# A's second score product cut to 64 rows, its two halves on opposite row groups of the array

## The chip, the cores and the metric

One NeuronCore of one Trainium2 chip runs the whole program. The metric is the device time of one execution in microseconds. A run of the same kernel is compared with other runs of it by their median; the profile is of one execution.

## What is computed

A trunk of two encoder layers over 1024 tokens of width 1024. Each layer projects the normalised input, runs three groups of attention heads side by side (A: six dense heads of 64 with two key heads, B: six windowed heads, C: four latent heads), gates their outputs and projects them back. The change lies in group A. Cut to what matters, the reference for it is

```python
def dense_gqa_blocks(q, k, v, scale):        # A: 6 query heads, 2 key heads, head dim 64
    qb = q.reshape(bsz, nb, BLOCK, n_kv, grp, d).transpose(1, 0, 2, 3, 4, 5)
    def one_block(q_blk):                    # 128 queries against all 1024 keys
        s = jnp.einsum('bqhgd,bkhd->bhgqk', q_blk, k).astype(jnp.float32) * scale
        p = jax.nn.softmax(s, axis=-1).astype(v.dtype)
        return jnp.einsum('bhgqk,bkhd->bqhgd', p, v)
```

All values are float32. The kernel splits each operand of a product into a high part in the type fp32r and a low part (what the high part leaves), and adds products of parts.

## The kernel before

**Stages.** Each layer has an input stage (projections, rotations, transposes; queries, keys and gates are written to DRAM), an attention stage, and an output stage. In the profile the attention stages lie at about 277 to 560 us (layer 0) and 921 to 1206 us (layer 1).

**Query stacks.** For group A and a tile of 128 queries, `qstack` (L767) loads one tile of 128 rows from DRAM (`qsta` in the trace) with four DMAs on SP's queue. Of each head, 64 rows hold the high part and the other 64 rows the low part; which half is which depends on whether the head is even or odd. The keys' high part (`ks["a", 0]`) and low part (`ks["a", 1]`, both `ka` in the trace) each hold the 64 rows of a key head twice, in the upper and the lower half.

**A unit.** `UnitA` (L894) is one head and one query tile: 8 query tiles x 2 key heads x 3 heads, 48 in a layer, 96 in all. Its `scores` (L899) handles the 1024 keys in two halves of 512. For a half, `mm3` (L133) issues two products that add up in one PSUM bank: the stack with the high keys (high x high + low x high) and the stack with the low keys (high x low + low x low). Both contract 128 rows. `softmax_unit` (L703) then lets DVE read the bank once (L711: copy with sign and running minimum), and after the second half ACT takes the exponential (L721). The transposes (L730), the split of the result (L737 to L742) and the product with the values (`pv`, L752) follow in later turns of the pipeline (L830).

**Buffers.** Three PSUM banks serve scores (`SBANKS`), four transposes, one the values. Gate tiles (`gt`, L807 and L1115) have `GBUFS` = 5 buffers, the tile `rb` (L791) two: `divided` (L778) makes the reciprocal sums, turns them, copies them to `rb` on ACT and multiplies them into the gate tile on POOL (L794).

**What sets the order.** The tile framework orders each engine's instructions by a timeline of its own, starting from priorities and dependences; `tc.keep_in_program_order` ties single instructions to the order in which they are written. SP's DMA queue is in order: an issue that waits for a buffer holds those behind it.

Of the kernel before, what the change touches and what calls it, by code (L numbers as in the profile page):

```python
# [8 lines left out]
F32 = mybir.dt.float32  # L9
F32R = mybir.dt.float32r  # L10
# [18 lines left out]
QAB = 4  # L29
QC = 4  # L30
OBUFS = 4
GBUFS = 5
C_AT = (2, 3, 5, 6, 8, 9, 11, 13)
WARM = 12
XBUFS = 6
# [10 lines left out]
def kernel(  # L46
# [21 lines left out]
    nc = tc.nc  # L68
    P = 128
# [14 lines left out]
    def after(ins, first):  # L84

        tc.add_manual_dep(
            ins,
            first.name,
            mybir.DependencyInfo(mybir.DependencyClass.NoSync, mybir.DependencyReason.DATA),
            reason="order",  # L90
        )
        return ins

    def dma(dst, src, eng=None):

        a, b = (t.bitcast(F32) if t.dtype == F32R else t for t in (dst, src))
        ins = (eng or nc.sync).dma_start(a, b)
        if queue_behind[0] is not None and eng is None:
            after(ins.ins, queue_behind[0])
        return ins.ins  # L100
# [3 lines left out]
    class Engine:  # L104


        def __init__(self, eng):
            self.eng = eng
# [16 lines left out]
    def rstd_of(ss, n, name, w):  # L125

        ms = small.tile([P, w], F32, tag=f"ms{w}", name=f"ms_{name}")
        V.tensor_scalar(ms, ss, 1.0 / n, EPS, ALU.mult, ALU.add)
        r = small.tile([P, w], F32, tag=f"rs{w}", name=f"rs_{name}")
        last_pow[0] = G.tensor_tensor(out=r, in0=ms, in1=mhalf[:, 0:w], op=ALU.pow).ins  # L130
        return r

    def mm3(ps, parts, first=True, last=True):  # L133

        for i, (a, b) in enumerate(parts):
            T.matmul(ps, lhsT=a, rhs=b, start=first and i == 0, stop=last and i == len(parts) - 1)  # L136
# [91 lines left out]
    for l in range(DEPTH):  # L228
        x_src = xin if l == 0 else x_next[l - 1]
        last = l == DEPTH - 1  # L230
# [4 lines left out]
        d_q = {g: dram.tile([NS, 2, P, 3, P], F32R, name=f"d_q{g}{l}") for g in "abc"}  # L235
# [11 lines left out]
        with stage.ph as ph:  # L247
# [6 lines left out]
            def ps_t(name):  # L254
                return ps1.tile([P, 512], F32, tag="T", name=name)
# [8 lines left out]
            def gemm_sc(ws, st, name):  # L264
                his, los, n = ws
                hf, c0 = st // 4, (st % 4) * P
                ps = ps_o(name)
                for dt in range(ND):
                    wh, wl = his[dt], los[dt]
                    h, lo = hTh[hf][:, dt, c0 : c0 + P], hTl[hf][:, dt, c0 : c0 + P]  # L270
                    mm3(ps[:, :n], [(h, wh), (h, wl), (lo, wh)], dt == 0, dt == ND - 1)
                return ps
# [144 lines left out]
            for st in range(NS):  # L417
                nm = f"{l}_{st}"
                ps = gemm_sc(ws, st, f"pza{nm}")
# [9 lines left out]
                r = rstd_of(ss, 1, f"a{nm}", 8)  # L429
# [31 lines left out]
            for st in range(NS):  # L461
                nm = f"{l}_{st}"
                ps = gemm_sc(ws_b, st, f"pzb{nm}")
# [218 lines left out]
        with ExitStack() as ph:  # L682
            ps2 = wa_.enter_context(tc.tile_pool(name=f"ps2_{l}", bufs=2, space=PSUM, reuse_waits="tile"))
            at = ph.enter_context(tc.tile_pool(name=f"at{l}", bufs=2, reuse_waits="tile"))
# [5 lines left out]
            pk = pk_.enter_context(tc.tile_pool(name=f"pk{l}", bufs=1, side="right", reuse_waits="tile"))  # L690
# [3 lines left out]
            def ps_s(name):  # L694
                return ps2.tile([P, 512], F32, tag="S", name=name, bufs=SBANKS)
# [4 lines left out]
            def ps_o(name):  # L700
                return ps2.tile([P, 512], F32, tag="O", name=name, bufs=OBANKS)

            def softmax_unit(half, sm, nm):  # L703


                nmx = [small.tile([P, 1], F32, tag=f"nmx{c}", name=f"nmx{nm}_{c}") for c in range(2)]
                p = at.tile([P, 1152], F32, tag="p", name=f"p{nm}", bufs=PBUFS)[:, 0:1024]
                for c in range(2):
                    ps = ps_s(f"s{nm}_{c}")
                    half(ps, c)  # L710
                    V.tensor_tensor_reduce(  # L711
                        p[:, c * 512 : (c + 1) * 512],
                        ps,
                        zero[:, 0:1].to_broadcast([P, 512]),
                        -1.0,
                        nmx[0][:, 0:1] if c else 3.0e38,
                        ALU.add,
                        ALU.min,
                        nmx[c],
                    )  # L720
                A.activation(p, p, AF.Exp, scale=-1.0, bias=nmx[1][:, 0:1], accum_out=sm)  # L721
                return p

            def transposed(p, pth, ptl, g, kts, nm, pool=True):

# [41 lines left out]
            def qstack(g, qt, nm):  # L767

                qcnt[0] += 1
                i = qcnt[0] % QAB  # L770
                t = (pk if i in (1, 2) else pq).tile([P, 6, P], F32R, tag=f"qst{i}", name=f"qst{nm}")
                t = t.rearrange("p (m a) s -> p m a s", a=2)
                for par, i in ((0, 0), (0, 1), (1, 0), (1, 1)):
                    r0 = 64 * (par ^ i)
                    ins = dma(t[r0 : r0 + 64, :, par, :], d_q[g][qt, i, 64 * par : 64 * par + 64])
                return t, ins

            def divided(gt, sums, n, nm):  # L778

                pr = ps_t(f"pr{nm}")  # L780
                rc = small.tile([P, 3, 2], F32, tag="rc", name=f"rc{nm}")
                V.reciprocal(rc[:, 0:n, :], sums)
                wide = at.tile([P, 384], F32, tag="rw", name=f"rw{nm}", bufs=1)
                G.tensor_copy(
                    wide[:, 0 : n * P].rearrange("p (m a d) -> p m a d", a=2, d=64),
                    rc[:, 0:n, :].unsqueeze(3).to_broadcast([P, n, 2, 64]),
                )
                for m in range(n):
                    ms = slice(m * P, (m + 1) * P)
                    T.transpose(pr[:, ms], wide[:, ms], ident)  # L790
                rb = at.tile([P, 384], F32, tag="rb", name=f"rb{nm}")  # L791
                A.copy(rb[:, 0 : n * P], pr[:, 0 : n * P])
                gv = gt.rearrange("p g s -> p (g s)") if len(gt.shape) == 3 else gt
                G.tensor_tensor(out=gv, in0=gv, in1=rb[:, 0 : n * P], op=ALU.mult)  # L794

            class Gqa:


                def __init__(self, g, qt, m0):
                    self.g, self.qt, self.m0 = g, qt, m0  # L800
                    self.nm = f"{g}{l}_{qt}"
                    self.q, self.loaded = qstack(g, qt, self.nm)
                    self.sm = small.tile([P, 6], F32, tag=f"sm{g}", name=f"sm{self.nm}", bufs=3)
                    self.o = at.tile([P, 3, P], F32, tag="o", name=f"o{self.nm}", bufs=OBUFS)

                def gate(self):
                    self.gt = qg.tile([P, 3, P], F32, tag="gt", name=f"gt{self.nm}", bufs=GBUFS)  # L807
                    dma(self.gt, d_gate[:, self.m0 : self.m0 + 3, self.qt * P : (self.qt + 1) * P])
# [13 lines left out]
                def divide(self):  # L822

                    divided(self.gt, self.sm.rearrange("p (m a) -> p m a", a=2), 3, self.nm)
# [55 lines left out]
            if True:  # L880
                ks, start = {}, {}
# [12 lines left out]
                class UnitA:  # L894
# [4 lines left out]
                    def scores(self):  # L899
                        a, kv, h = self.a, self.kv, 3 * self.kv + self.g  # L900

                        def half(ps, c):
                            cs = slice(c * 512, (c + 1) * 512)
                            mm3(ps, [(a.head(h), ks["a", 0][:, kv, cs]), (a.head(h), ks["a", 1][:, kv, cs])])

                        self.p = softmax_unit(half, a.sm[:, h : h + 1], self.nm)

                    def turn(self):
                        if self.g == 0:
# [180 lines left out]
            class GroupC:  # L1090
# [23 lines left out]
                def gate(self):  # L1114
                    self.gt = qg.tile([P, 384], F32, tag="gt", name=f"gt{self.nm}", bufs=GBUFS)  # L1115
                    dma(self.gt[:, 0 : self.n], d_gate[:, 6 + self.hp, self.q0 * P : self.q1 * P])
# [9 lines left out]
            class UnitC:  # L1126
# [5 lines left out]
                def scores(self):  # L1132
                    ks, par, t = self.c.ks, self.par, self.c.qts[self.g]

                    def half(ps, c):
                        cs = slice(c * 512, (c + 1) * 512)
                        stack, mixed = t[:, 0, par, :], t[:, 1, par, :]
                        mm3(ps, [(stack, ks.k1[:, par, cs]), (mixed, k2[:, par, cs]), (mixed, k3[:, cs])])

                    self.p = softmax_unit(half, self.c.sm[:, par, self.g : self.g + 1], self.nm)  # L1140
# [75 lines left out]
        with ExitStack() as ph:  # L1216
# [10 lines left out]
            for st in range(NS):  # L1227
                nm = f"{l}_{st}"
# [4 lines left out]
                for c in range(2):  # L1233
                    cs = slice(c * 512, (c + 1) * 512)
                    for _ in out_part(st, c, MW if (st, c) in wa_.ps else 0, 8):
                        pass
                    ps = wa_.ps[st, c]
# [16 lines left out]
                if last:  # L1254
                    ms = small.tile([P, 1], F32, tag="ms1", name=f"ms_f{nm}")
                    V.scalar_tensor_tensor(ms, ss[:, 1:2], 1.0 / D, e0, ALU.mult, ALU.add)
                    r = small.tile([P, 1], F32, tag="rs1", name=f"rs_f{nm}")
# [93 lines left out]
```

## Time and profile before

| what | value |
|---|---|
| median of 3 runs | 1325.95 us (1325.19 to 1326.66) |
| the profiled execution | 1325.05 us |
| its span, first to last instruction | 1323.3 us |
| PE busy | 1294.8 us, 98% |
| DVE, ACT, POOL busy | 67%, 54%, 40% |
| mean granted clock of TensorE | 0.996 of full speed |

The page gives for one execution how long each engine was busy, and for groups of instructions the time of one and what ended the idle time before it. PE is the matrix engine, PEld its weight loads, which run beside products. A record of a product runs from its start to its modelled end; the next product may start before that end, so the distance of two starts (the step) is told from the timeline or the chain, not from a record's length. The chain of waits follows the work that ended last back through what released it.

### The profile page before, as it was taken

The numbers are of one execution on the slowest core, as the hardware profiler recorded it, in microseconds if no ns is written. First come the engines' busy times: TensorE is split into PE (matmuls) and PEld (weight loads), VectorE is DVE, ScalarE is ACT, GpSimd is POOL, SyncE is SP. The second block draws the span as 40 slices with busy tenths as digits, with TensorE's granted clock in tenths as the row PEclk, the third lists the DMA queues.
The fourth block names the chain that finished last, engine by engine and source line by source line (L and its number), as shares of the span: only waits on it lengthen the run. The fifth ranks groups of instructions, "written<-read, shape, count | busy, mean of one in ns | idle before, by whom it ended". The sixth has DMA issues, their size and how long they took to land.

```text
span 1323.3 us, 21690 instructions
## 1 busy us (share of the span) xinstructions
PE 1294.8 (98%) x7320; PEld 1131.1 (85%) x7320; DVE 882.6 (67%) x2242; ACT 720.7 (54%) x1551; POOL 530.2 (40%) x602
## 2 busy tenths in 40 slices
PE   7999999999999999999999999999999999999997
PEld 7888998878998998878898889888798988888786
DVE  5685662058888988875537766600888899888543
ACT  4332341168888898842323224311888889887332
POOL 3430121026766666751114101200367776677210
PEclk8999999999999999999999999999999999999999
DMA  7244469255211431345523345791742226114443
GB/s 255 89 125 150 136 203 258 89 140 142 82 49 56 115 90 47 108 144 177 186 91 115 121 134 157 237 221 55 180 102 61 72 64 149 38 40 148 147 146 115
DMA packets 174702, 166.46 MB, mean 126 GB/s; under 512 B 22400, under 2 KB 147200, under 8 KB 174592
## 3 DMA queue, kind: packets, MB, share of 16 engines
q1 hardware_dynamic: 155840, 140.43, 37.3%
q10 hardware_dynamic: 18752, 24.65, 5.4%
q8 instruction: 58, 0.95, 0.3%
q14 instruction: 52, 0.43, 0.1%
HBM read 107.35 MB, written 57.67 MB: 125 GB/s over the span
## 4 chain that ended last, share of the span: by engine, by line
PE 84%; DVE 5%; ACT 4%; DMA 3%; issue 2%; POOL 1%; SPq 1%; POOLq 0%; DVEq 0%; ACTq 0%
PE pg L136 13%; PE pw L136 12%; PE pzb L114 7%; PE pza L114 7%; PE poa L136 6%; PE ppa L730 5%; PE pzc L136 5%; PE sa L136 5%; PE sc L136 4%; PE ppc L730 4%; PE poc L136 3%; PE sb L136 2%; PE pob L136 2%; PE pzv L114 2%; PE pzv L136 2%
## 5 line engine op out<-in xcount | busy, mean ns | idle before, releaser
L711 DVE CUSTOM_DVE_ANT_0 pa<-sa,zero 128x512 f32<-128x512 f32 x96 | 65.5, 682 | 140.2 <-PE sa L136 137.1
L738 POOL TENSOR_SCALAR ptha<-pfa 128x512 fp32r<-128x512 f32 x96 | 59.8, 624 | 207.8 <-ACT pfa L737 199.7
L739 POOL TENSOR_TENSOR ptla<-pfa,ptha 128x512 fp32r<-128x512 f32 x96 | 124.1, 1293 | 5.7
L136 PE MATMUL sa<-ka,qsta 128*128 128x512 f32 x384 | 124.5, 418 | 1.4 <-DVE nmxc L711 0.7
L721 ACT ACTIVATE pa<-pa,nmxa 128x1024 f32<-128x1024 f32 x96 | 111.4, 1161 | 8.8 <-DVE nmxa L711 8.8
L136 PE MATMUL sc<-k,qc 128*128 128x512 f32 x384 | 113.2, 411 | 0.0
L730 PE MATMUL ppa<-ident,pa 128*128 128x128 f32 x768 | 106.5, 273 | 0.2
L730 PEld LDWEIGHTS ppa<-ident,pa 128*128 128x128 f32 x768 | 91.5, 141 | 15.1 <-DVE ptlb L742 0.6
L136 PE MATMUL pw<-woh,oh 128*128 128x512 f32 x256 | 98.9, 395 | 3.4 <-ACT oh L1029 2.6
L136 PE MATMUL pg<-hTh,wh 128*128 128x512 f32 x256 | 100.4, 392 | 0.0
L136 PE MATMUL pg<-hTh,wl 128*128 128x512 f32 x256 | 100.1, 391 | 0.0
L136 PE MATMUL pg<-hTl,wh 128*128 128x512 f32 x256 | 100.1, 391 | 0.0
L136 PE MATMUL pw<-wol,oh 128*128 128x512 f32 x256 | 99.7, 392 | 0.1
L136 PE MATMUL pw<-woh,ol 128*128 128x512 f32 x256 | 97.9, 393 | 0.3 <-DVE ol L1030 0.3
L644 ACT ACTIVATE g<-pg 128x512 f32<-128x512 f32 x32 | 19.1, 598 | 137.3 <-PE pg L136 107.0
L218 POOL TENSOR_SCALAR wh<-wst 128x384 fp32r<-128x384 f32 (+1 forms) x52 | 30.6, 607 | 145.5 <-PE pzb L114 79.2
L136 PE MATMUL poa<-ptha,vAB 128*128 128x384 f32 x256 | 88.0, 344 | 0.9 <-POOL ptla L739 0.3
L136 PE MATMUL poa<-ptla,vAB 128*128 128x384 f32 x256 | 86.5, 338 | 0.0
L721 ACT ACTIVATE pc<-pc,nmxc 128x1024 f32<-128x1024 f32 x64 | 74.0, 1156 | 8.2 <-DVE nmxc L711 8.0
L136 PEld LDWEIGHTS sc<-k,qc 128*128 128x128 f32 x384 | 66.3, 189 | 8.6
L711 DVE CUSTOM_DVE_ANT_0 pa<-sa,zero,nmxa 128x512 f32<-128x512 f32 x96 | 71.2, 744 | 3.4 <-PE sa L136 0.7
L730 PE MATMUL ppc<-ident,pc 128*128 128x128 f32 x512 | 71.9, 273 | 1.5 <-ACT pfc L737 0.8
(234 smaller groups left out, 3812.6 us busy)
## 6 DMA issues: line engine op xcount, KB each, us to landing
wst<-in_w_in_dram SPq DMA_DIRECT2D x20, 512.0 KB, 3.7
d_gate<-g ACTq DMA_DIRECT2D x32, 256.0 KB, 2.0
wost<-in_w_out_dram SPq DMA_DIRECT2D x32, 256.0 KB, 2.7
wst<-in_w_in_dram SPq DMA_DIRECT2D x16, 384.0 KB, 4.2
qsta<-d_qa SPq DMA_DIRECT2D x64, 96.0 KB, 2.8
qstb<-d_qb SPq DMA_DIRECT2D x64, 96.0 KB, 2.8
k<-d_kn SPq DMA_DIRECT2D x12, 512.0 KB, 7.0
qc<-d_qc SPq DMA_DIRECT2D x96, 64.0 KB, 2.2
```

The costliest lines, as they stand in the source:

```text
L114: return lambda *a, **k: tc.keep_in_program_order(f(*a, **k))
L136: T.matmul(ps, lhsT=a, rhs=b, start=first and i == 0, stop=last and i == len(parts) - 1)
L218: G.tensor_scalar(h, f, 1.0, 0.0, ALU.mult, ALU.add)
L644: A.activation(g, ps, AF.Silu)
L711: V.tensor_tensor_reduce(p[:, c * 512 : (c + 1) * 512], ps, zero[:, 0:1].to_broadcast([P, 512]), -1.0, nmx[0][:, 0:1] if c else 3.0e38, AL ...
L721: A.activation(p, p, AF.Exp, scale=-1.0, bias=nmx[1][:, 0:1], accum_out=sm)
L730: T.transpose(pt[:, (j - q0) * P : (j - q0 + 1) * P], p[:, j * P : (j + 1) * P], ident)
L738: G.tensor_scalar(hi, f, 1.0, 0.0, ALU.mult, ALU.add)
L739: G.tensor_tensor(out=lo, in0=f, in1=hi.bitcast(F32), op=ALU.subtract)
```

## The change

The second product of a half keeps only the high rows of the query: 64 rows against the low keys (low x low is left out). The first half of the keys takes the rows where the head's high part lies in the old stack. The second half takes the other 64 rows, for which a second tile, `other` (`qota` in the trace), holds the high parts of the odd and even heads in exchanged halves; two more DMAs per query tile load it, into one of two buffers. Both halves' banks are taken first, and the four products are issued in the order high, high, low, low and tied to it. To make room, gate tiles have four buffers and `rb` one.

```diff
-GBUFS = 5
+GBUFS = 4
...
-            def softmax_unit(half, sm, nm):
+            def softmax_unit(half, sm, nm, both=None):
...
+                if both:
+                    pss = [ps_s(f"s{nm}_{c}") for c in range(2)]
+                    both(pss)
                 for c in range(2):
-                    ps = ps_s(f"s{nm}_{c}")
-                    half(ps, c)
+                    if both:
+                        ps = pss[c]
+                    else:
+                        ps = ps_s(f"s{nm}_{c}")
+                        half(ps, c)
...
+            def ordered(ps, a, b, first, last):
+                tc.keep_in_program_order(nc.tensor.matmul(ps, lhsT=a, rhs=b, start=first, stop=last))
...
-                rb = at.tile([P, 384], F32, tag="rb", name=f"rb{nm}")
+                rb = at.tile([P, 384], F32, tag="rb", name=f"rb{nm}", bufs=1)
...
+                    if g == "a":
+
+                        self.other = pk.tile([P, 3, P], F32R, tag=f"qot{qt % 2}", name=f"qot{self.nm}")
+                        for par in range(2):
+                            r0 = 64 - 64 * par
+                            dma(self.other[r0 : r0 + 64], d_q[g][qt, 0, 64 * par : 64 * par + 64])
...
-                        def half(ps, c):
-                            cs = slice(c * 512, (c + 1) * 512)
-                            mm3(ps, [(a.head(h), ks["a", 0][:, kv, cs]), (a.head(h), ks["a", 1][:, kv, cs])])
-
-                        self.p = softmax_unit(half, a.sm[:, h : h + 1], self.nm)
+                        def both(pss):
+                            cs = [slice(c * 512, (c + 1) * 512) for c in range(2)]
+                            hi, lo = ks["a", 0], ks["a", 1]
+                            for c in range(2):
+                                ordered(pss[c], a.head(h), hi[:, kv, cs[c]], True, False)
+
+                            for c, stack in enumerate((a.head(h), a.other[:, h // 2, :])):
+                                r = slice(64, 128) if (h + c) % 2 else slice(0, 64)
+                                ordered(pss[c], stack[r], lo[r, kv, cs[c]], False, True)
+
+                        self.p = softmax_unit(None, a.sm[:, h : h + 1], self.nm, both)
```

On PE, query tile 4 of layer 0, key head 0, second head of its group, before (a name is stage, tile, key head, head, half and a running number; `ka` with the smaller number is the high part of the keys, and the 512 columns of the result stand last):

```order
L730 MATMUL ppb_3_1_1_0_4721<-ident,scb_3_1_4652 128x128 x3
L136 MATMUL sa_4_0_1_0_4816<-ka_0_2789,qsta_4_4751 128x512
L136 MATMUL sa_4_0_1_0_4816<-ka_0_2792,qsta_4_4751 128x512
L136 MATMUL sa_4_0_1_1_4820<-ka_0_2789,qsta_4_4751 128x512
L136 MATMUL sa_4_0_1_1_4820<-ka_0_2792,qsta_4_4751 128x512
L136 MATMUL sb_4_0_0_4860<-kb_0_2802,qstb_4_4758 128x384
```

and with the change:

```order
L799 MATMUL pra_3_4817<-ident,rwa_3_4820 128x128 x3
L731 MATMUL sa_4_0_1_0_4831<-ka_0_2792,qsta_4_4763 128x512
L731 MATMUL sa_4_0_1_1_4832<-ka_0_2792,qsta_4_4763 128x512
L731 MATMUL sa_4_0_1_0_4831<-ka_0_2795,qsta_4_4763 128x512
L731 MATMUL sa_4_0_1_1_4832<-ka_0_2795,qota_4_4768 128x512
L136 MATMUL poa_3_1_2_4859<-ptha_3_1_0_1_4639,vAB_90 128x384
```

The four products now go high, high, low, low, and the last reads the second tile; other units' work around them moved too. Over the program the two 64-row products stand directly behind each other in 94 of 96 units.

On SP's queue, where the attention of layer 0 begins, before:

```order
L97 DMA qsta_0_2782<-d_qa_78 64x3x128 x4
L97 DMA ka_0_2789<-d_ka_81 64x2x1024 x2
L97 DMA ka_0_2792<-d_ka_81 64x2x1024 x2
L97 DMA qstb_0_2795<-d_qb_79 64x3x128 x4
L97 DMA kb_0_2802<-d_kb_82 64x2x1024 x2
```

and with the change, there and, farther on, at query tile 3:

```order
L97 DMA qsta_0_2782<-d_qa_78 64x3x128 x4
L97 DMA qota_0_2787<-d_qa_78 64x384 x2
L97 DMA ka_0_2792<-d_ka_81 64x2x1024 x2
...
L97 DMA qota_3_4281<-d_qa_78 64x384 x2
L97 DMA qstb_3_4286<-d_qb_79 64x3x128 x3
L97 DMA qc_0_6_4963<-d_qc_80 64x2x128 x2
```

The first two loads of the new tile stand between the query stack and the keys; those of tile 3 stand ahead of loads for groups B and C.

## Rows read from the trace of the kernel before

**Rows 1.** The page: span, share of each engine, and the granted clock in 40 slices.
```profile
span 1323.3 us, 21690 instructions
...
PE 1294.8 (98%) x7320; PEld 1131.1 (85%) x7320; DVE 882.6 (67%) x2242; ACT 720.7 (54%) x1551; POOL 530.2 (40%) x602
...
PEclk8999999999999999999999999999999999999999
```

**Rows 2.** Windows of both attention stretches: length, busy us (x instructions) of each engine, clock, DMA.
```profile
core 0: us, PE busy (x) PEld busy (x) DVE busy (x) ACT busy (x) POOL busy (x), PEclk, DMA share, GB/s
277.00:560.00 283.00, 279.15 (x1749) 248.76 (x1748) 247.84 (x691) 244.89 (x529) 186.66 (x208) 1.00 0.35 91
921.00:1206.00 285.00, 280.99 (x1751) 250.15 (x1750) 242.07 (x682) 241.00 (x521) 184.60 (x205) 1.00 0.33 86
```

**Rows 3.** Tile sa: ns min/median/max, first and last start in us.
```profile
L136 PEld LDWEIGHTS sa<-ka,qsta x384: 186/189/192, 277.0 to 1179.6; 128*128 128x128 f32 x192
L136 PE MATMUL sa<-ka,qsta x384: 387/397/504, 277.2 to 1179.8; 128*128 128x512 f32 x192
L711 DVE CUSTOM_DVE_ANT_0 pa<-sa,zero x96: 649/682/693, 277.9 to 1179.6; 128x512 f32<-128x512 f32 x96
L711 DVE CUSTOM_DVE_ANT_0 pa<-sa,zero,nmxa x96: 731/745/754, 279.2 to 1181.6; 128x512 f32<-128x512 f32 x96
```

**Rows 4.** Timeline around the first attention product: start us, us, engine.
```profile
276.34 0.39 PE L136 MATMUL pg<-hTh,wl 128*128 128x512 f32 x1
276.34 0.19 PEld L136 LDWEIGHTS pg<-hTh,wh 128*128 128x128 f32 x1
276.57 0.39 PE L136 MATMUL pg<-hTh,wh 128*128 128x512 f32 x1
276.57 0.19 PEld L136 LDWEIGHTS pg<-hTl,wh 128*128 128x128 f32 x1
276.79 0.39 PE L136 MATMUL pg<-hTl,wh 128*128 128x512 f32 x1
276.80 0.19 PEld L136 LDWEIGHTS pg<-hTh,wl 128*128 128x128 f32 x1
```

**Rows 5.** Chain of waits, in order of time, of a piece of layer 0's attention.
```profile
427.22 0.46 PE sa L136 x2
...
428.73 0.47 PE sa L136 x2
...
429.54 0.87 PE ppc L730 x8
...
435.25 0.47 PE sa L136 x2
435.72 0.44 PE ppa L730 x4
436.16 0.69 PE sc L136 x3
```

**Rows 6.** Chain of waits by line, in 277 to 560 and in 921 to 1206 us.
```profile
by line: PE poa L136 14.7%; PE ppa L730 10.6%; PE sa L136 10.0%; PE sc L136 9.4%; PE ppc L730 8.0%; PE poc L136 4.6%; PE pob L136 4.5%; DVE pa L711 4.5%; PE sb L136 4.3%; issue 3.4%; PE ppb L730 2.6%; ACT pa L721 2.5%; ACT scb L969 2.2%; DV
...
by line: PE poa L136 15.5%; PE sa L136 11.8%; PE ppa L730 11.6%; PE sc L136 9.0%; PE ppc L730 7.4%; PE poc L136 5.9%; PE sb L136 4.8%; PE pob L136 4.5%; DVE pa L711 3.4%; PE ppb L730 3.2%; PE pg L136 2.5%; issue 2.2%; ACT pa L721 1.6%; DVE 
```

**Rows 7.** Waits of PE in 277 to 560 us: us in total, times, longest.
```profile
PE sb L136 <- DVE nmxa L711: 1.8, 5, 1.0
PE sa L136 <- DVE nmxc L711: 0.4, 1, 0.4
```

**Rows 8.** The page's DMA issues: KB each, us to landing.
```profile
qsta<-d_qa SPq DMA_DIRECT2D x64, 96.0 KB, 2.8
```

**Rows 9.** Tile qsta: its loads as issued on SP's queue.
```profile
L97 SPq DMA_DIRECT2D qsta<-d_qa x64: 512/605/754, 207.1 to 1116.1; - x64
```

**Rows 10.** Tile ka: its loads as issued on SP's queue.
```profile
L97 SPq DMA_DIRECT2D ka<-d_ka x8: 585/605/618, 210.5 to 863.3; - x8
```

**Rows 11.** Waits of SP's queue in 277 to 560 us.
```profile
SPq L97 <- POOL ob L827: 54.7, 7, 14.7
```

**Rows 12.** Tiles gta and rba: gate loads, the copy, the multiplication that reads both.
```profile
L97 SPq DMA_DIRECT2D gta<-d_gate x16: 377/487/1307, 240.7 to 1134.1; - x16
L794 POOL TENSOR_TENSOR gta<-gta,rba x16: 1003/1016/1030, 306.9 to 1198.9; 128x384 f32<-128x384 f32 x16
...
L792 ACT COPY rba<-pra x16: 467/485/523, 306.2 to 1197.4; 128x384 f32<-128x384 f32 x16
```

## The prediction

> **What bounds the kernel now.** I read the page first. TensorE (PE) is busy for 1294.8 of 1323.3 us, 98%; the next engine, VectorE (DVE), for 67% [rows 1]. [...] The change acts in the two attention stretches alone, so I read the windows of those: PE busy 279.15 of 283 us and 280.99 of 285 us, with DVE at 248 and 242 us and ScalarE (ACT) at 245 and 241 us, 85 to 88% [rows 2]. Two more engines stand close behind PE there.
>
> A busy PE says little of what one product is worth, since the records overlap: a score product of A is recorded with 397 ns (median) and its weight load with 189 ns [rows 3], yet in the timeline one 512-column product starts every 0.22 to 0.23 us, and the weight load of the next starts with it and lies beside it [rows 4]. The price of a product is therefore its step, not its record. The chain of waits gives the same: two A products take 0.47 us, so 0.235 each, and eight transposes 0.87 us, so 0.109 each with a weight load of their own [rows 5].
>
> Last, how much of A's product time lies on the path. The chain by line in the two stretches has A's scores (sa) at 10.0% of 283 us and 11.8% of 285 us, 28.3 + 33.6 = 61.9 us [rows 6]. All 384 products at 0.235 us are 90.2 us. So 69% of this work is on the chain; the rest lies beside pieces that DVE, ACT or an issue ends. What PE waits for by name is small, at most 1.8 us in a row of the waits [rows 7].
>
> **The change, part by part.**
>
> *Four steps become three.* Before, a unit (one head, 128 queries, 1024 keys) has two halves of two products. There are 96 units (96 reductions of each half, [rows 3]), so 384 products. After, it still has 384 products and 384 weight loads, but the two second ones of a unit use 64 rows each, on opposite halves of the array, into different banks. If they run side by side, a unit loses one step of 0.235 us. They stand directly behind each other in 94 of 96 units: 94 x 0.235 = 22.1 us of PE time.
>
> No row of this trace shows a 64-row product, so I bound it. More than one step cannot be gained: three passes of 512 columns are left, and no row shows one with a shorter step than 0.22 us. The other end: no overlap, the array running empty before and after the pair (record minus step, 397 - 235 = 162 ns each time) and a weight load of 109 ns not hidden each time: 2 x 271 ns x 96 = +52 us. I take the gaining end, because the nearest row, the back-to-back stream [rows 4], shows that PE starts a product as soon as weights and columns are there, and here neither rows, nor banks, nor a semaphore holds the second one. Weight loads have room: four at 0.109 us are 0.44 us under three steps of 0.705 us.
>
> [...]
>
> *How much of it reaches the end.* Between 69% (the chain's share) and 100% (PE is busy for 98.6% of the stretches). I take 0.8, nearer to the chain's share, since DVE and ACT at 85 to 88% would rise to about 90% in a stretch 9 us shorter. 22.1 x 0.8 = 17.7 us; ends 15.2 and 22.1.
>
> *The order high, high, low, low.* Now a first reduction can start after three steps where it could after two, and the second follows it at once. Per unit: before, 0.47 us of products, then 0.682 + 0.745 us of reductions [rows 3] (the second half's products, done at 0.94 us, hide behind the first reduction); after, 0.705 us and the same reductions. Each unit's exponential comes 0.235 us later. Other products and transposes cover that, except where the chain runs through these reductions: DVE pa has 4.5% and 3.4% of the two stretches [rows 6], 12.7 + 9.7 = 22.4 us, which is 16 units at 1.43 us. 16 x 0.235 = 3.8 us is the upper end, 0 the lower; I take 1 us, since the order was laid anew around it. A unit also holds two of three score banks at once; that is in the same upper end.
>
> *Two more loads per query tile.* 16 query tiles x 2 issues of 96 KB, like those of qsta, which take 2.8 us to land [rows 8] and 0.605 us to issue [rows 9]. That is 32 x 0.605 = 19 us of SP's queue and 3 MB of 166 MB. The queue has room: in the first stretch alone it waits 54.7 us for one kind of store [rows 11]. The first of them stand behind qsta and ahead of ka: qsta and ka are issued from 207 and 210 us [rows 9, 10], the first score product starts at 277 [rows 3], so 1.2 us more is covered by 60. The later ones have two buffers, so a load waits for the last unit of the tile two before, and in the order rows qc and qstb stand behind it on the queue. Those are needed a query tile later, some 35 us (283 us over 8 tiles). Taken at 0. If that cover went, a late landing would cost up to 2.8 us on each of 14 tiles, 39 us; nothing in the rows points to it.
>
> *Four gate buffers, one rb.* The first gate tile is loaded from 240.7 us and first used at 306.9 [rows 12]; one buffer fewer eats into 66 us of lead. The rb copy (485 ns) would wait for the multiplication of the one before (1016 ns [rows 12]), which ended many microseconds earlier: 16 of A over both stretches is one in 35 us. Both 0.
>
> Sum: 1325.05 - 17.7 + 1.0 = 1308.4 us against the profiled execution (span 1323.3 plus 1.75 around it). The median of the runs shown is 0.9 us above that execution, so I forecast **1309 us**; the forecast's own range is 1303 to 1313.
>
> **The rivals.**
>
> *A. The second of the pair waits for its weights.* In all the rows shown a load starts with the product before its own, one ahead and not two [rows 4]. If that always holds, the second 64-row product starts one load, 0.109 us, behind the first; a pair gives 0.126 us, and 94 x 0.126 x 0.8 - 1 = 8.5 us: 1317 us. For it: the rows never show two ahead. Against: they have full-height loads alone, for which there is no free half.
>
> *B. Slower: the array runs empty at each change of height.* A pair stands between 128-row products, so there are two changes per unit. If nothing starts until the last product is out, each costs 397 - 235 = 162 ns at both edges of the pair: +0.324 - 0.235 = +0.089 us per pair, 94 of them 8.4 us, with 1 us for the order: 1334 us. The point from which it decides is 0.118 us a change. For it: each record has 0.16 us of tail to lose. Against: going from products to transposes, another kind of work on the array, costs nothing in the chain (two products 0.47 us, four transposes 0.44, three products 0.69, one behind the other [rows 5]). If the pair moreover doesn't overlap it is 96 x 0.324 + 1 = 32 us, 1357 us, the far tail of this case.
>
> [...]
>
> *C. The change doesn't do what it says.* The two run one after the other, each with a step of its own, and no change costs anything. PE's time stays, the order's 1 us is left: 1326 us.
>
> *D. Another engine takes over.* PE gets its 22 us, but DVE and ACT hold the stretches, and a quarter comes through: -5.5 + 1 = 1320.5 us. For it: 85 to 88% busy. Against: PE's own idle time is only 8 us of 568 now.
>
> **How the numbers follow.** Forecast 0.42, A 0.17, B 0.23, C 0.12, D 0.06. A measurement of this kernel tells about 0.2%, 2.7 us, from no change. Faster by more: forecast, A and D less 0.04 for a smaller A or D, 0.61. Within: that 0.04 and most of C, 0.12. Slower: B and what is left of C, 0.27. Range 1303 to 1337: from the forecast's best end to a little past B; left out are B's far tail (about 0.08) and a better gain than one step (0.03).
>
> **What would show it.** In the changed profile: right, if the two 64-row products of a unit start within some 10 ns of each other, the next product starts about 0.235 us after them, and the two stretches are 7 to 11 us shorter each. A shows as a start 0.11 us behind. B shows as more than 0.3 us between the last 128-row product and the pair, or behind it. C shows as 0.235 us between the two. D shows as a PE with gaps that reductions or ACT end. The forecast is wrong if the time is above 1313 us; the reasoning is wrong if it is below 1303.

## The result, and the profile after

| | before | with the change |
|---|---|---|
| median | 1326.31 us (4 runs, 1325.19 to 1327.38) | 1462.7 us (4 runs, 1461.79 to 1467.17) |
| ratio | 1 | 1.1036, 95% interval 1.1022 to 1.1051 |
| span of the profiled execution | 1323.3 us | 1461.2 us |

The change makes the kernel 136 us slower. The forecast was 1309 us, the range ended at 1337.

The page of the changed kernel: span, engines, granted clock in 40 slices, and the chain by engine.

```profile
span 1461.2 us, 21779 instructions
...
PE 1350.4 (92%) x7320; PEld 1128.6 (77%) x7320; DVE 877.8 (60%) x2242; ACT 726.2 (50%) x1551; POOL 528.6 (36%) x602
...
PEclk9999999879999999999999999996899999999999
...
PE 72%; DVE 9%; ACT 7%; DMA 5%; issue 4%; POOL 1%; SPq 0%; POOLq 0%; DVEq 0%; ACTq 0%
```

The chain by engine in the kernel before:

```profile
PE 84%; DVE 5%; ACT 4%; DMA 3%; issue 2%; POOL 1%; SPq 1%; POOLq 0%; DVEq 0%; ACTq 0%
```

PE's busy time rose by 56 us against [rows 1], but its share fell from 98 to 92%, and the chain, 84% on PE before, is on PE for 72% only. So PE both works longer and waits. The clock row has two dips, at slices 8 to 9 and 28 to 29, where it had nines: where each attention stage begins.

The windows of the changed kernel, the start of each attention stage apart from the rest; the columns are those of [rows 2].

```profile
core 0: us, PE busy (x) PEld busy (x) DVE busy (x) ACT busy (x) POOL busy (x), PEclk, DMA share, GB/s
277.00:310.00 33.00, 16.87 (x50) 10.21 (x51) 9.03 (x30) 9.62 (x21) 3.77 (x4) 0.55 1.00 219
310.00:640.00 330.00, 299.53 (x1746) 243.51 (x1745) 244.85 (x674) 242.72 (x516) 195.28 (x216) 0.99 0.30 83
1000.00:1030.00 30.00, 15.70 (x47) 9.60 (x48) 8.42 (x27) 8.33 (x20) 3.76 (x4) 0.51 0.95 203
1030.00:1360.00 330.00, 300.15 (x1753) 245.49 (x1751) 247.05 (x677) 243.25 (x517) 195.66 (x216) 0.98 0.31 84
```

The windows of [rows 2] cut the stages only roughly (the second begins 7 us before layer 1's gate products end). From the last gate product to the first product of the output stage (pw), the start times in the traces give 287 us before and 365 us now, in both layers. The output stages are 8 to 9 us shorter, since less of the attention's own work reaches into them (18 us past the first pw product, 28 before); 2 x 78 less 17 us is about the 138 us between the spans.

Before, PE was idle for 4 us of each stage [rows 2]. Now, in the first 30 us, PE is busy half the time, the DMA engines are full (1.00 and 0.95) and the granted clock averages 0.55 and 0.51. The trace's clock records have two values, 1.0 and 0.5 of full speed; they stand at 0.5 from 280 to 311 us and from 1001 to 1031 us. In the 330 us that follow PE has 30 us of idle time at a DMA share of 0.30. These are two separate losses.

The first one. The loads of the keys (tile ka) as issued on SP's queue, and what that queue waited for from 200 to 300 us:

```profile
L97 SPq DMA_DIRECT2D ka<-d_ka x8: 573/605/620, 277.5 to 999.0; - x8
```

```profile
SPq L97 <- PE pg L136: 38.1, 1, 38.1
SPq L97 <- DMA d_gate<-g: 29.6, 1, 29.6
```

The first ka load is issued at 277.5 us; it was 210.5 [rows 10]. Ahead of it the queue stood still for 38.1 + 29.6 = 68 us, in waits that a gate product (pg) and the store of a gate (d_gate) ended.

What PE waited for in layer 0's attention stage (us in total, times, longest):

```profile
PE sa L731 <- DMA ka<-d_ka: 11.0, 2, 10.0
PE pob L136 <- DVE ptlb L751: 5.3, 8, 1.1
PE sb L136 <- DMA kb<-d_kb: 4.0, 2, 2.1
PE pob L136 <- ACT pthb L750: 3.4, 3, 1.5
PE ppb L739 <- ACT pfa L746: 2.5, 2, 1.5
```

[Rows 7] had 1.8 us at most. The keys (ka, kb) are the first loss. The clock belongs to it: it falls in the 10.0 us in which PE waits for the first ka load (276.3 to 286.3 us), and stays at 0.5 of full speed for the next 25 us; the transposes in them follow each other at 0.21 us, where it is 0.11 later. The other waits come from the softmax chain: the split of the transposes (ptlb, pthb, pfa) that DVE and ACT make. The chain by line in the steady part answers to [rows 6]:

```profile
by line: PE poa L136 13.6%; PE sa L731 7.6%; issue 7.4%; PE ppa L739 6.5%; PE poc L136 5.6%; DVE pa L717 5.5%; PE sc L136 4.4%; ACT pa L727 3.8%; DVE pc L717 3.6%; ACT pc L727 3.5%; DVE ptlb L751 3.0%; PE pob L136 2.8%; PE sb L136 2.8%; PE 
```

PE lines have shrunk, and issue (7.4%), DVE pa, ACT pa, DVE pc, ACT pc and DVE ptlb stand among them, each a handover from one engine to the next.

A third thing to read is the pair itself. The products of tile sa, then one pair in the timeline:

```profile
L731 PE MATMUL sa<-ka,qsta x288: 387/480/796, 286.3 to 1323.4; 128*128 128x512 f32 x96, 64*128 64x512 f32 x48
...
L731 PE MATMUL sa<-ka,qota x96: 491/498/791, 290.6 to 1324.1; 64*128 64x512 f32 x96
```

```profile
439.55 1.48 PE L731 MATMUL sa<-ka,qsta 128*128 128x512 f32 x3
...
440.11 0.19 PEld L731 LDWEIGHTS sa<-ka,qsta 128*128 128x128 f32 x1 [0.40 <-DVE nmxa L717]
...
440.53 0.18 PEld L731 LDWEIGHTS sa<-ka,qsta 64*128 64x128 f32 x1 [0.24 <-issue]
440.53 0.18 PEld L731 LDWEIGHTS sa<-ka,qota 64*128 64x128 f32 x1
440.54 0.50 PE L731 MATMUL sa<-ka,qota 64*128 64x512 f32 x1
...
440.96 0.19 PEld L136 LDWEIGHTS poc<-pthc,vC 128*128 128x128 f32 x1 [0.25 <-issue]
440.97 0.45 PE L136 MATMUL poc<-pthc,vC 128*128 128x384 f32 x1
441.07 0.19 PEld L136 LDWEIGHTS poc<-ptlc,vC 128*128 128x128 f32 x1
441.25 0.34 PE L136 MATMUL poc<-ptlc,vC 128*128 128x384 f32 x1
```

The row at 439.55 holds three products: the two full-height ones and the first of the pair. Both weight loads of 64 rows are issued at 440.53, the second product (qota) starts at 440.54. Over the 94 pairs the two starts lie 3 ns apart (median), so the pair does run side by side. But its weights are loaded only when it starts, and the full-height load behind it only at 440.96, 0.43 us after the pair's start, where [rows 4] have the next load start with each product. The product at 440.97 then takes 0.28 us to the next one, where a 384-column step without a height change is 0.17 (441.25 to 441.43 in the same stretch of the trace).

Medians over the 94 pairs, from the starts: 0.33 us from the full product before the pair to the pair, 0.43 us from the pair to the next, and 0.10 us more on that one's step. Less the full product's own step (0.23 us at 512 columns), a pair takes 0.63 us. Two plain steps are 0.46. So the pair loses 0.17 us, and an entry with its exit costs 0.63 - 0.23 = 0.40 us.

### The profile page after: what moved, and what is told of

Its sections match the earlier page's. It is cut to its first block, busy times and chain, and to the rows that moved or that the text cites. A ratio compares the mean times of both kernels' runs of the same rounds, so it can differ in the third digit from the quotient of the medians.

```text
span 1461.2 us, 21779 instructions
## 1 busy us (share of the span) xinstructions
PE 1350.4 (92%) x7320; PEld 1128.6 (77%) x7320; DVE 877.8 (60%) x2242; ACT 726.2 (50%) x1551; POOL 528.6 (36%) x602
## 4 chain that ended last, share of the span: by engine, by line
PE 72%; DVE 9%; ACT 7%; DMA 5%; issue 4%; POOL 1%; SPq 0%; POOLq 0%; DVEq 0%; ACTq 0%
PE pg L136 12%; PE pw L136 10%; PE poa L136 6%; PE pzb L114 6%; PE pza L114 6%; PE pzc L136 4%; PE sa L731 4%; PE ppa L739 4%; PE poc L136 3%; PE sc L136 3%; DVE pa L717 2%; PE ppc L739 2%; PE pob L136 2%; DMA kb<-d_kb 2%; PE pzv L114 2%
## 5 line engine op out<-in xcount | busy, mean ns | idle before, releaser
L731 PE MATMUL sa<-ka,qsta 128*128 128x512 f32 (+1 forms) x288 | 126.0, 475 | 24.8 <-DMA ka<-d_ka 21.8
L739 PE MATMUL ppa<-ident,pa 128*128 128x128 f32 x768 | 110.6, 288 | 5.2 <-ACT pa L727 2.8
L731 PEld LDWEIGHTS sa<-ka,qsta 128*128 128x128 f32 (+1 forms) x288 | 55.5, 200 | 62.4 <-issue 50.1
L751 DVE TENSOR_TENSOR ptla<-ppa,ptha 128x512 fp32r<-128x512 f32 x96 | 65.7, 686 | 25.4 <-ACT ptha L750 24.9
```

What stands on the lines that cost most here:

```text
L731: tc.keep_in_program_order(nc.tensor.matmul(ps, lhsT=a, rhs=b, start=first, stop=last))
L739: T.transpose(pt[:, (j - q0) * P : (j - q0 + 1) * P], p[:, j * P : (j + 1) * P], ident)
L751: V.tensor_sub(lo, ptv, hi.bitcast(F32))
```

## The experiments

Three theories were to be told apart. P: the tie to the written order keeps scores from running ahead. L: the larger pool of keys makes the first loads late. E: the array runs empty at each change of height. Kernels that have the 64-row products (e1, e5, e7, e8, e9, e11) leave out low x low as the change does; the others have it.

| run | median us | against the kernel before (95%) |
|---|---|---|
| the change | 1462.7 | 1.1036 (1.1022 to 1.1051) |
| e1, first product free | 1387.0 | 1.0469 (1.0439 to 1.0499) |
| e2, before, tied | 1406.0 | 1.0603 (1.0584 to 1.0621) |
| e3, before, memory side alone | 1387.9 | 1.0468 (1.0449 to 1.0487) |
| e4, the change on 128 rows | 1459.1 | 1.101 (1.099 to 1.103) |
| e5, e1 with the loads placed anew | 1344.7 | 1.0137 (1.0122 to 1.0151) |
| e6, e5 on 128 rows | 1331.3 | 1.0038 (1.0025 to 1.005) |
| e7, four 64-row products in a row | 1338.3 | 1.0088 (1.0074 to 1.0103) |
| e8, e5 with four score banks | 1346.2 | 1.0143 (1.0122 to 1.0164) |
| e9, before, single 64-row products | 1380.2 | 1.0386 (1.037 to 1.0401) |
| e10, before, small buffers | 1327.2 | 0.9993 (0.9981 to 1.0005) |
| e11, the change with the loads placed anew | 1429.1 | 1.076 (1.0744 to 1.0777) |

The kernel before ran at 1326.8, 1326.6 and 1327.6 us beside the three groups (e1 to e4, e5 to e8, e9 to e11).

**e1: the first product of a unit free.**

```diff
-                                ordered(pss[c], a.head(h), hi[:, kv, cs[c]], True, False)
+                                ordered(pss[c], a.head(h), hi[:, kv, cs[c]], True, False, c == 1)
```

(the last argument of `ordered` says whether to tie)

> The changed kernel, with the first of a unit's four products no longer tied to the place where it is written; the other three stay tied behind it. Theory P (the tie keeps a unit's scores from running ahead of the softmax work of the unit before, so PE waits on DVE and ACT): the steady part of attention, 310 to 640 us in the changed kernel, shrinks by some 40 us a layer, so 1463 - 80 = about 1380 us, and the start of attention still loses about 25 us a layer. Rival E (the array runs empty at the change of height and that alone is the loss): nothing is gained, 1455 to 1465 us. Rival L (the late loads are the whole of it): no gain either.

Measured 1387.0 us, a little above the 1380 expected: one tie less a unit gives back 76 us. P holds; E and L alone do not.

**e2: the kernel before with A's scores tied.**

```diff
-                            mm3(ps, [(a.head(h), ks["a", 0][:, kv, cs]), (a.head(h), ks["a", 1][:, kv, cs])])
+                            for i in range(2):
+                                tc.keep_in_program_order(
+                                    nc.tensor.matmul(
+                                        ps, lhsT=a.head(h), rhs=ks["a", i][:, kv, cs], start=i == 0, stop=i == 1
+                                    )
+                                )
```

> The kernel before, with 128 rows, old order and old buffers; only A's score products are tied to the place where they are written. Theory P: 1326 + 70 to 90 = about 1400 us. Rival E and rival L: 1326 us within 5, since nothing runs empty and no load is moved.

Measured 1406.0 us, 79 us above the kernel before, with no 64-row product and no load moved. Its windows (columns of [rows 2]) and waits of PE in attention:

```profile
277.00:605.00 328.00, 298.57 (x1792) 260.75 (x1791) 250.76 (x700) 249.76 (x537) 196.85 (x217) 0.98 0.31 84
922.00:1282.00 360.00, 330.62 (x1911) 285.46 (x1910) 237.62 (x675) 244.91 (x529) 185.08 (x205) 0.99 0.28 76
```

```profile
PE poa L136 <- DVE ob L820: 4.8, 7, 1.1
PE pob L136 <- DVE ptlb L742: 2.9, 2, 2.2
PE ppa L730 <- ACT pa L721: 2.7, 6, 0.6
PE ppc L730 <- DVE ptlc L742: 2.6, 3, 1.1
```

The second window takes in the last 44 us of layer 1's gate products, in which PE doesn't wait. The keys are not among the waits; PE is idle for 29 us in each stage, and what ends the waits is again DVE and ACT. The reason can be counted in the order of the products in the traces, taking each at its plain step (0.227 us for 512 columns, 0.175 for 384, 0.120 for 256, 0.109 for a transpose, the median distances of starts in the kernel before): between a unit's last score product and its first transpose stand 8.8 us of other PE work (median of 96 units) in the kernel before, 3.7 in the changed kernel, 3.5 in e2, 7.3 in e1. In between lie two reductions and one exponential, 0.682 + 0.745 us [rows 3] and 1.161 us (the exponential's mean in the kernel before), plus whatever DVE and ACT have queued before them, and both are 85 to 88% busy. By this count 9 us of lead cover that and 4 do not. e1 and e2 show that the tie is the cause; that the lost lead is the way is read from these counts and the waits.

**e3: the kernel before with the memory side of the change.**

```diff
-GBUFS = 5
+GBUFS = 4
...
+                    if g == "a":
+
+                        self.other = pk.tile([P, 3, P], F32R, tag=f"qot{qt % 2}", name=f"qot{self.nm}")
+                        for par in range(2):
+                            r0 = 64 - 64 * par
+                            dma(self.other[r0 : r0 + 64], d_q[g][qt, 0, 64 * par : 64 * par + 64])
```

(and `rb` with one buffer)

> The kernel before with only the memory side of the change: the second query tile is there and loaded but nobody reads it, four gate buffers, one rb. Theory L (the pool of keys grows by 3072 B a partition, so its lowest tile, the first query stack, falls onto the gate weights, and the loads of keys wait behind it on SP's queue until those weights are done): both attention stages start about 25 us late, 1326 + 50 = about 1376 us, with the first ka load issued at about 277 us and not 210. If the loads do not matter: 1326 us within 3.

Measured 1387.9 us, 61 us lost where 50 were expected. The first load of ka, and the chain where layer 0's attention starts:

```profile
L97 SPq DMA_DIRECT2D ka<-d_ka x8: 603/606/607, 278.8 to 962.5; - x8
```

```profile
269.98 5.00 PE pg L136 x22
...
275.00 0.56 SPq L97
...
280.80 11.12 DMA ka<-d_ka
...
291.94 11.58 DMA kb<-d_kb
...
303.56 0.61 PE sb L136 x2
```

Issued from 278.8 us, the keys of A land at 292, those of B at 303.5. Two 1.5 KB tiles and their loads are not the cost (e6 below has them too and is 4.7 us slower in all); the place is. The pool `pk` ends at a fixed address, so growing it by 3072 B a partition lowers its first tile, the query stack qsta: in the layout of the built programs it goes from byte 172480 of a partition to 169408, and the low parts of the gate weights (wl) end at 170944. Its load waits for late gate products, which read these weights, and everything behind it on SP's queue waits with it: the queue stands still for 38.1 + 29.6 us here too.

**e4: the change with 128 rows.**

```diff
-                            for c, stack in enumerate((a.head(h), a.other[:, h // 2, :])):
-                                r = slice(64, 128) if (h + c) % 2 else slice(0, 64)
-                                ordered(pss[c], stack[r], lo[r, kv, cs[c]], False, True)
+                            for c in range(2):
+                                ordered(pss[c], a.head(h), lo[:, kv, cs[c]], False, True)
```

> The changed kernel with its order, ties and buffers, but the two last products of a unit contract all 128 rows again (low x low comes back; the second query tile is loaded and not read). Four steps a unit, no change of height. From the trace of the changed kernel a pair costs 0.33 us to enter, 0.43 us to leave and one weight load of 0.11 us that is not hidden, 0.87 us against 0.69 us for three plain steps: 0.18 us x 94 = 16 us at most. Theory E small: 1463 - 16 x 0.7 = about 1450 us. If running empty were the main loss: below 1400 us. If the pair were a gain: above 1463 us.

Measured 1459.1 us: 3.6 us faster by the medians, though the intervals (1.099 to 1.103 and 1.1022 to 1.1051) overlap, and less than the 13 us expected. The height is not the main loss; what it costs hardly shows while PE waits anyway. Hence e5 and e6.

**e5: e1 with the second tile below the keys, its first load last.**

```diff
-                    if g == "a":
+                    if g == "a" and qt:
+                        self.load_other()
...
+                def load_other(self):
+                    qt = self.qt
+                    self.other = pq.tile([P, 3, P], F32R, tag=f"qot{qt % 2}", name=f"qot{self.nm}")
...
                 start["a"].gate()
                 start["b"].gate()
+                start["a"].load_other()
```

> The kernel of e1 (64-row pairs, first product of a unit free), and the second query tile moved into the pool that lies below the keys, its first load issued behind the keys, the mask and the gates. Nothing of the first loads then waits for the gate weights. Theory L: the 61 us that the memory side cost in e3 come back, 1387 - 55 to 61 = 1326 to 1332 us, the first ka load issued at about 210 us. If something else of the memory side (four gate buffers, one rb) is behind a part of the 61 us, it stays: above 1340 us.

Measured 1344.7 us, 42 us less than e1, not the 55 to 61 expected: a miss by 13 us in size. By its own condition (above 1340 us) that pointed at the small buffers; e10 below finds them worth nothing. The loads are back in their old place:

```profile
L97 SPq DMA_DIRECT2D ka<-d_ka x8: 574/605/607, 210.2 to 871.9; - x8
```

**e6: e5 on 128 rows** (the edit of e4).

> e5 with the last two products of a unit on all 128 rows again (low x low comes back), order high, high, low, low. Against e5 it tells the worth of the pair where PE is the bound. By the starts in the changed kernel's trace a pair costs 0.18 us net: 94 x 0.18 x (0.7 to 1) = 12 to 17 us faster than e5. By my forecast the pair gains: 15 to 22 us slower than e5. If change of height and gain cancel: within 4 us.

Measured 1331.3 us, 13.4 us faster than e5. With little else in the way the 64-row pairs lose, 0.14 us each over the 96, a little under the 0.17 of the starts. Some 2 us of the 13.4 are not theirs: in e5 PE waits 2.4 us for loads of the second tile, which e6 doesn't read. e6 is the kernel before plus the order high, high, low, low, three ties within a unit, the loads and the small buffers: 4.7 us slower.

**e7 and e8: four 64-row products in a row, and its reference.** e8 is e5 with `SBANKS = 4` and `TBANKS = 3`. e7 adds

```diff
...
+                        todo = [(3 * kv + self.g, pss)]
+                        if self.partner:
+                            self.partner.pss = [ps_s(f"s{self.partner.nm}_{c}") for c in range(2)]
+                            todo.append((3 * kv + self.g + 1, self.partner.pss))
...
+                        for n, (h, banks) in enumerate(todo):
+                            for c in range(2):
+                                ordered(banks[c], a.head(h), hi[:, kv, cs[c]], True, False, n or c)
+                        for h, banks in todo:
+                            for c, stack in enumerate((a.head(h), a.other[:, h // 2, :])):
+                                r = slice(64, 128) if (h + c) % 2 else slice(0, 64)
+                                ordered(banks[c], stack[r], lo[r, kv, cs[c]], False, True)
```

> e8 with the first two heads of a group together: four high products, then four 64-row products in a row, so 32 of the 96 entries and exits go while the number of pairs stays. If each entry and exit together costs 0.40 us (0.10 to enter, 0.31 to leave, with a weight load that is not hidden): 32 x 0.40 x (0.7 to 1) = 9 to 13 us faster than e8. If the loss of a pair does not sit at the change of height: within 3 us of e8.

> e5 with four score banks and three transpose banks, the reference for e7. If two score banks held by one unit were a bottleneck: 5 us or more faster than e5. If the transposes need their four banks: slower than e5. Otherwise within 4 us of it.

e8 measured 1346.2 us, within 2 us of e5: a fourth score bank, taken from the transposes, gains nothing. e7 measured 1338.3 us, 7.9 us faster than e8, a little under the 9 to 13 expected: the four stand together in 26 groups, not in all 32. One of them in e7's timeline:

```profile
408.67 0.90 PE L731 MATMUL sa<-ka,qsta 128*128 128x512 f32 x2
409.09 0.72 PE L731 MATMUL sa<-ka,qota 64*128 64x512 f32 x2
409.43 0.39 PE L731 MATMUL sa<-ka,qsta 64*128 64x512 f32 x1
409.75 0.96 PE L741 MATMUL ppa<-ident,pa 128*128 128x128 f32 x6
```

The row at 408.67 again ends with the first 64-row product. At 409.09 two start together, then two more (the second product of the row at 409.09 and the one at 409.43), and the next full work follows at 409.75: one entry and one exit for four products.

In this place the step before needs care. A 512-column product right behind a transpose starts 0.03 us after it, where a step between transposes is 0.11, and the product behind it 0.32 us later instead of 0.23 (medians over 219 such places in the kernel before): 0.08 us are only moved from one step to the next. So it is in 22 of the 26 groups. Counted from one product farther back, less plain steps, the 26 groups take 0.82 us (median), four plain steps 0.91; the pairs of e8, counted so, take 0.63. So by the starts one pair loses 0.17 us and two pairs in a row gain 0.09. For the 26 groups that makes 26 x (2 x 0.63 - 0.82) = 11 us against e8, of which 7.9 reached the end. No run has groups of four alone, so that they gain in the kernel's time is not shown. By the same count six in a row would gain 0.31 us (0.82 + 0.23, against 1.36), but they need six score banks of the eight that the kernel gives out (three, four and one); that was not tried. No version here beats the kernel before.

**e9: single 64-row products in the old order.**

```diff
-                            mm3(ps, [(a.head(h), ks["a", 0][:, kv, cs]), (a.head(h), ks["a", 1][:, kv, cs])])
+                            r = slice(64, 128) if h % 2 else slice(0, 64)
+                            mm3(ps, [(a.head(h), ks["a", 0][:, kv, cs]), (a.head(h)[r], ks["a", 1][r, kv, cs])])
```

> The kernel before, same order on PE, same buffers and loads; each second product of A contracts the 64 high rows alone (low x low left out), and none stands beside another: 180 single ones and 6 pairs of them in a row. In the changed kernel's trace a 64-row product that stands alone takes 0.62 us from the product before it to the product behind it, where a plain step is 0.23. If the change of height is the price: 186 x 0.39 x (0.7 to 1) = 51 to 73 us slower than before, 1378 to 1400 us. If only a pair were dear (two banks, two weight loads): within 5 us of before.

Measured 1380.2 us, 52.6 us slower, within the 51 to 73 expected, 0.28 us for each of 186 places. Less work, same order, no second tile: the change of height alone. Its window of layer 0's attention (columns of [rows 2]) and one such product in the timeline:

```profile
277.00:600.00 323.00, 321.32 (x1825) 258.32 (x1823) 260.68 (x710) 254.89 (x543) 200.26 (x221) 1.00 0.33 87
```

```profile
436.87 0.40 PE L136 MATMUL sc<-k,qc 128*128 128x512 f32 x1
437.11 0.82 PE L136 MATMUL sa<-ka,qsta 128*128 128x512 f32 x2
437.86 0.50 PE L136 MATMUL sc<-k,qc 128*128 128x512 f32 x1
438.21 0.60 PE L730 MATMUL ppa<-ident,pa 128*128 128x128 f32 x4
```

PE counts as busy for 321.32 of 323 us: nothing in the busy share shows this loss, the steps do. The row at 437.11 holds a full and a 64-row product; from its start to 437.86 are 0.75 us where two steps are 0.46, and the next step takes 0.35 where it is 0.23. That is 0.41 us for this one; the median of those with two full products before them is 0.40, or some 75 us over the 186, more than the 52.6 measured. The rest takes the place of waits: beyond the plain steps of its products an attention stage has 13 us in the kernel before and 38 us in e9, nearly all of them at 64-row products, and 2 x (38 - 13) is about what was measured.

**e10: small buffers alone.**

```diff
-GBUFS = 5
+GBUFS = 4
...
-                rb = at.tile([P, 384], F32, tag="rb", name=f"rb{nm}")
+                rb = at.tile([P, 384], F32, tag="rb", name=f"rb{nm}", bufs=1)
```

> The kernel before with four gate buffers and one rb, nothing else. It tells what of the 4.7 us between e6 and the kernel before comes from the buffers. My prediction took both at 0: within 2 us of before. If they make the gates wait: 3 to 6 us slower.

Measured 1327.2 beside 1327.6 us: nothing, as predicted.

**e11: the change with the loads of e5** (all four products tied).

> The changed kernel with all four products of a unit tied, as it stands, but with the second query tile placed and loaded as in e5. If the ties and the loads add up: 1463 less the 42 us by which e5 is faster than e1, 1420 us, give or take 8, with the attention stages starting at once. If one hides behind the other: above 1440 us.

Measured 1429.1 us, 1 us outside what was expected. Between e11 and e5 only the tie of the first product differs, 84 us; between e11 and the change only the place and time of the loads, 34 us. So the tie is worth 76 to 84 us in three comparisons, the loads 34, 42 and 61. Why the loads cost less where 64-row pairs and ties are present than in e3 was not separated. The clock goes with them: at the starts of the two attention stages it is at 0.5 of full speed for 31 us each in the change and in e1, for 24 and 31 us in e3, and for 3 to 7 us in e5 and e11.

## Why the prediction was wrong

- **What bounds the kernel: right.** PE is the bound; every loss found here is PE waiting or taking longer steps where the height changes.
- **Four steps become three, 17.7 us of gain: wrong in sign.** The pair does run side by side, 3 ns apart, so the overlap was right. What failed is the choice of the gaining end: the bound on the other side, a loss at both edges of the pair, was the true one. Its size in case B, 0.162 us an edge, 0.324 for both, was near: 0.40 us were measured, 0.10 of them the longer step behind the pair, whose weight load starts with its product. The traces show the longer steps; that the array runs empty in them is my reading and not shown. Net 0.17 us a pair by the starts where case B had 0.089, and 13.4 us in e5 against e6 where it had 8.4. The share of a gain that reaches the end, taken at 0.8 with 0.69 as its lower end, was near: of what the starts give, 11 to 13 of 16 us reached the end in e5 against e6, 52.6 of 75 in e9 and 7.9 of 11 in e7 against e8. Case A (weights one ahead) is refuted, the two loads go together; so is case C.
- **The argument against case B** was that going from products to transposes costs nothing in the chain. That change keeps the full height, so it said nothing about this one.
- **The order high, high, low, low, taken at 1 us, at most 3.8: the step that failed most.** I priced the later reduction and read the tie as an order within a unit. It also ties the unit's first product behind whatever is written before it on PE, and so ends the run-ahead of scores: 79 us (e2), 76 us (e1). The order itself, without that tie, is at most the 4.7 us of e6. The prediction held D, the softmax engines taking over, at 0.06 and as a limit to a gain; the mechanism that came is its reverse: DVE and ACT are no busier (877.8 and 726.2 us, where the kernel before has 882.6 and 720.7), PE comes to them too late.
- **Two more loads, taken at 0 because 60 us of lead covered them: failed.** The lead was real and was lost: the lead hung on where the pool lies, and the prediction looked at the queue alone. 34 to 61 us. It also did not reckon with the clock: the mean was 0.996 of full speed in the kernel before and is 0.970 with the keys late, 0.55 and 0.51 over the starts of the two attention stages.
- **Buffers at 0: right** (e10).
- Two sums are slightly off and decide nothing: the terms of the forecast's own range give 1304 to 1314.6 us where it has 1303 to 1313, and case B's 1334 lacks the 0.9 us between the profiled execution and the median that the forecast adds.

Parts against the whole: the tie 79 (e2), the memory side 61 (e3) and the height 3.6 (e4) sum to 144 us for the 136 measured. The losses overlap: where PE waits anyway the height costs 3.6 us (the change against e4), with little else in the way 13.4 (e5 against e6). Taken off one after another, the loads are 34 us (to e11), the tie 84 (to e5), the height 13 (to e6), and 5 are left.

## What to carry to other kernels

Price 64-row products by the passage from the last full-height product to the full rhythm behind them, not by their number: by the starts a pair between full-height work loses 0.17 us and two pairs in a row gain 0.09, so gather them or leave them. Before tying an instruction to the written order, ask what stands written before it on that engine and how many microseconds of run-ahead go with it. Before adding a tile to a pool, look at which addresses the first tiles move to and who still uses them: here the load of the query stack, which had to wait, held those behind it on SP's queue for 68 us.

## What was not expected of the hardware

- In e9 a 64-row product that stands alone costs more than a full one, 0.28 us at each of 186 places: e9 does less arithmetic than the kernel before and is 3.9% slower.
- The weight load behind a pair does not go ahead: in the changed kernel the load of the full-height product starts 0.43 us after the pair (median of the 94), with that product, while [rows 4] have it 0.2 us ahead.
- In the changed kernel a wait of 10 us for the keys is followed by 25 us at 0.5 of the clock (records from 280 to 311 us; averages of 0.55 and 0.51 over the starts of the two stages), with transposes at 0.21 us a step where it is 0.11 later: PE is also slower behind the stall.
